# Two float32r parts in place of one float32 matmul for GpSimd's sum of exponentials, issued one step later

## The chip, the cores and the metric

One core of a Trainium2 chip. The metric is device time in microseconds (us); the kernel before has a median of 3220.47 us over 3 runs (3214.39 to 3221.25). TensorE is called PE, VectorE DVE, ScalarE ACT, GpSimd POOL, and the queue that issues the transfers SP. Each engine works its own queue in order.

## The reference, cut to what matters

A hybrid encoder layer for 2048 prompt tokens and 512 sample tokens, width 1024. One input projection feeds two attention mixers of 8 heads each: branch A (grouped-query, head size 64) and branch B (latent attention, 64 + 32). Both attend without a mask inside their own group of tokens:

```
s = jnp.einsum('bqgrd,bkgd->bgrqk', qblk, k, preferred_element_type=jnp.float32) * scale
p = jax.nn.softmax(s, axis=-1).astype(v.dtype)
return jnp.einsum('bgrqk,bkgd->bqgrd', p, v)
```

The two results are gated, projected, merged, projected once more, normalised and added to x. All of it is float32. Softmax needs, for each query, the sum of its exponentials over all keys: this sum is what the change is about.

## The kernel before, in words

Three stages follow one another: `in_proj` (about 1160 us), `attention` (to about 2750 us) and `tail`. The change touches `attention` alone.

**Float32 from float32r.** TensorE's float32r form rounds its operands. So the kernel splits a float32 operand into a rounded high part and a low part, the difference, and multiplies the parts in several matmuls. ScalarE makes the high part (a copy whose output is float32r), VectorE or GpSimd subtracts to get the low one.

**Jobs and steps.** Attention is 80 jobs: branch by branch, head by head, and in each head four chunks of 512 prompt queries and one chunk of 512 sample queries. A prompt job has 2048 keys, cut into 16 key tiles of 128; a *step* takes two of them, so a prompt job has 8 steps (n = 0 to 7) and a sample job 2. In each step:

- PE writes the scores of the step's two key tiles into a PSUM tile `st` (line 980; two matmuls per key tile in branch A, three in branch B). `st` has two buffers.
- ACT writes `ph`, the rounded exponential, to SBUF (line 983; a ring of six buffers), and then the full exponential back into `st` (line 984).
- DVE subtracts the two into `pl`, the low part (line 993). That frees `st`.
- PE also computes scores for a coming job into `mp` (line 947, one buffer), and DVE takes their maximum (line 950): the maximum has to be known before a job's own exponentials.
- Two to three steps later PE multiplies `ph` and `pl` with the values (`values`, lines 1003 and 1004) into the PSUM tiles `X` and `Y` of the job, one buffer each. `values` for the last key tile of a job stands in the next job's second step, and for the first tiles in a job's own fourth step.

**The sum of the rounded weights.** Y's row 64 collects the sums over keys. The low parts come in through a column of ones in the value tile (line 1004). The rounded parts of pairs n = 0 to 6 are added by POOL: six adds of 128x1024 into `acc` (line 986) and one that adds the two halves of `acc` (line 988). They enter Y through one float32 matmul with a selector, `sel[0]` (line 1008), right behind the job's last values. The last pair, n = 7, is summed by PE itself with the float32r selector `sel[1]` (line 1006, two matmuls). Sample jobs use line 1006 for all their tiles and have no `acc`.

**The end of a job.** `finish` has ACT copy X and Y to SBUF (lines 1015 and 1016); POOL then adds the two halves of X's copy (line 1027, tile `xa`) and, after a transfer, a second piece (line 1029, tile `s`). `later(k, f)` posts work k steps on.

**What sets the order.** From the first job on, the order of PE, ACT, DVE, POOL and SP is the order in which the Python loop at the end of `attention` emits the instructions: in each step first `scores`, then the values that have come due with one step of the maximum stream (`advance`) among them, then what `later` has due, then `lows`, then the POOL add that `finish` returned.

Of the kernel before, what the change touches and what calls it, by code (L numbers as in the profile page):

```python
# [9 lines left out]
F32 = mybir.dt.float32  # L10
F32R = mybir.dt.float32r
AF = mybir.ActivationFunctionType
ALU = mybir.AluOpType
# [4 lines left out]
P = 128  # L18
# [5 lines left out]
CH = 512  # L24
# [119 lines left out]
VW = 130  # L144
# [614 lines left out]
def attention(tc, nc, env, h4):  # L759
    e = NS(env)  # L760
    dma, nm, f32 = e.dma, e.nm, e.f32
    ha, fl, filler, cur, rest = h4
    kp = Pool(tc, "kp", "left")
# [21 lines left out]
    def zero_q(pool):  # L785
        qz = pool.tile([P, CH], F32R, name=nm("qz"))
        nc.vector.memset(f32(qz), 0.0)
        qzs.append(qz)

    zero_q(kp)  # L790
    zero_q(kp)
    sel = [kp.tile([P, VW - 64], t, name=f"sel{n}") for n, t in enumerate((F32, F32R))]
    for a in (sel[0], f32(sel[1])):
        nc.vector.memset(a, 0.0)
        nc.vector.memset(a[:, 64:VW - 64], 1.0)
    tops = [[kp.tile([P, 32], F32, name=f"m{s}{n}") for s in "pt"] for n in range(3)]
    for m, _ in tops:
        nc.vector.memset(m, 0.0)
# [35 lines left out]
    def post_now(out, in_):  # L834
        dma(f32(out), in_)
# [7 lines left out]
    def start(i, br, h, c):  # L843

        j = Job()
        j.br, j.h, j.c = br, h, c
        j.last = (br, h, c) == specs[-1]
        smp = int(c == 4)
        j.nk = (NS_TOK if smp else NP_TOK) // P
        j.direct = 0 if smp else j.nk // 2 - 1  # L850
        j.k1, j.k2, j.vt = kcur[(*kv_of(br, h), smp)]
        j.k3 = k3s[smp]
        qn, qr = q_src(br, h, c)
        j.qz = qzs[i % 3]
        j.qm = kp.tile([P, CH], F32R, tag="qm", name=nm("qm"), bufs=4)
        if br == 0:
            dma(f32(j.qm), qn[0].partition_broadcast(2))
            j.km = j.k1
            j.scale = SC_A
        else:  # L860
            dma(f32(j.qm[0:64, :]), qn[0])
            dma(f32(j.qm[64:128, :]), qr[0].partition_broadcast(2))
            j.km = j.k2
            j.scale = SC_B
        j.mx = kp.tile([P, 4, 2], F32, tag="mx", name=nm("mx"), bufs=3)
        return j
# [15 lines left out]
    at = Pool(tc, "at", "left")  # L882
# [35 lines left out]
    jobs = []  # L918
# [7 lines left out]
    def due(last=False):  # L926
        while queue and (last or queue[0][0] <= clock[0]):
            queue.pop(0)[2]()
# [37 lines left out]
            later(1, row)  # L966
            yield True

    def scores(j, n):

        if n == 0:
            if j.direct:
                j.acc = at.tile([P, 2, CH], F32, tag="acc", name=nm("acc"), bufs=2)
            j.hs, j.ls = [], []
        st = pp.tile([P, 2, CH], F32, tag="st", name=nm("st"), bufs=2)
        for a in range(2):
            kt = 2 * n + a
            ps = j.passes(j, slice(kt * P, (kt + 1) * P))
            for i, (k, q) in enumerate(ps):
                nc.tensor.matmul(st[:, a, :], lhsT=k, rhs=q, start=(i == 0), stop=(i == len(ps) - 1))  # L980
        h = at.tile([P, 2, CH], F32R, tag="ph", name=nm("ph"), bufs=6)
        j.hs.append(h)
        nc.scalar.activation(out=h, in_=st, func=AF.Exp, scale=j.scale)  # L983
        nc.scalar.activation(out=st, in_=st, func=AF.Exp, scale=j.scale)  # L984
        if 0 < n < j.direct:
            nc.gpsimd.tensor_tensor(out=j.acc, in0=f32(j.hs[0]) if n == 1 else j.acc, in1=f32(h), op=ALU.add)  # L986
            if n == j.direct - 1:
                nc.gpsimd.tensor_tensor(out=j.acc[:, 0, :], in0=j.acc[:, 0, :], in1=j.acc[:, 1, :], op=ALU.add)
        return st

    def lows(j, st):
        l = at.tile([P, 2, CH], F32R, tag="pl", name=nm("pl"), bufs=4)
# [3 lines left out]
    def values(j, kt):  # L996

        if kt == 0:
            j.X, j.Y = x_bank(), y_bank()
        n, a = kt // 2, kt % 2  # L1000
        y = j.Y[0:VW - 64, :]
        st, sp = kt == 0, kt == j.nk - 1
        nc.tensor.matmul(j.X, lhsT=j.vt[:, kt, 0:P], rhs=j.hs[n][:, a, :], start=st, stop=sp)  # L1003
        nc.tensor.matmul(y, lhsT=j.vt[:, kt, 64:VW], rhs=j.ls[n][:, a, :], start=st, stop=False)  # L1004
        if n >= j.direct:
            nc.tensor.matmul(y, lhsT=sel[1], rhs=j.hs[n][:, a, :], start=False, stop=sp and not j.direct)  # L1006
        if sp and j.direct:
            nc.tensor.matmul(y, lhsT=sel[0], rhs=j.acc[:, 0, :], start=False, stop=True)  # L1008
        return j if sp else None

    def finish(j):

        y = at.tile([VW - 64, CH], F32, tag="y", name=nm("ys"), bufs=2)
        xa = at.tile([P, CH], F32, tag="xa", name=nm("xa"), bufs=2)
        nc.scalar.copy(out=xa, in_=j.X)  # L1015
        nc.scalar.copy(out=y, in_=j.Y[0:VW - 64, :])
        later(1, lambda: dma(e.sums[j.br][j.c, j.h:j.h + 1, :], y[64:65, :]))
        if j.h == 7 and not j.last:
            for k, step in enumerate(inverse(nc, e, at, j.br, j.c)):
                later(6 + 2 * k, step)  # L1020
        if (j.br, j.h, j.c) == (1, 7, 0):
            for k, step in enumerate(tail_load(nc, e, wt, 1, 0, first_y)):
                later(13 + 3 * k, step)

        def rest():
            s = at.tile([64, CH], F32, tag="s", name=nm("s"), bufs=2)
            nc.gpsimd.tensor_tensor(out=xa[0:64, :], in0=xa[0:64, :], in1=y[0:64, :], op=ALU.add)
            later(1, lambda: dma(s, xa[64:128, :]))
            later(3, lambda: nc.gpsimd.tensor_tensor(out=s, in0=s, in1=xa[0:64, :], op=ALU.add))
            later(5, lambda: dma(  # L1030
                e.o_s[j.br][j.h // 2, 64 * (j.h % 2):64 * (j.h % 2) + 64, j.c * CH:(j.c + 1) * CH], s))

        return rest
# [4 lines left out]
    def advance(to):  # L1038
        while done[0] < to and next(stream, None) is not None:
            done[0] += 1  # L1040

    steps = [(i, n) for i, m in enumerate(pairs) for n in range(m)]
# [3 lines left out]
    with contextlib.ExitStack() as order:  # L1046
# [14 lines left out]
        passes = {0: start_main(0, *specs[0])}  # L1061
        order.close()
        order.enter_context(tc.manual_schedule(engines={eng.PE, eng.Activation, eng.DVE, eng.Pool, eng.SP}))
        ready, g = [], -1
        while g + 1 < len(steps) or ready:
            g += 1
            clock[0] = g
            st, rest = None, None
            if g < len(steps):
                i, n = steps[g]  # L1070
                br, h, c = specs[i]
                if c < 2 and n == 4:
                    late = [0]

                    def post_later(out, in_):
                        later(late[0], lambda: post_now(out, in_))
                        late[0] += 1

                    if c == 0 and i + 5 < len(specs):
                        load_k(*kv_of(*specs[i + 5][0:2]), 0, post_later)  # L1080
                    if c == 1:
                        load_k(*kv_of(br, h), 1, post_later)
                if n == 0:
                    for k in range(i + 1, min(i + 3, len(specs))):
                        if k not in passes and (k == i + 1 or pairs[i + 1] < 8):
                            passes[k] = start_main(k, *specs[k])
                    jobs[i].passes = passes.pop(i)
                    if specs[i] == (1, 0, 0):
                        for k in range(4):
                            later(24 * k + 4, lambda k=k: wa.append(load_raw(nc, e, wt, e.a_out, k)))  # L1090
                            later(24 * k + 12, lambda k=k: wa.append(
                                split_raw(nc, e, wt, "wa", wa.pop(), k, nc.gpsimd)))
                        for m, step in enumerate(tail_load(nc, e, wt, 0, 0, first_y)):
                            later(24 * m + 100, step)
                        later(180, lambda: y0.extend(split_y(nc, e, wt, 0, first_y.pop())))
                st = scores(jobs[i], n)
                ready += [(g + BACK + (n == 0), jobs[i], 2 * n + a) for a in range(2)]
            now = sum(r[0] <= g for r in ready)
            for m in range(min(now, 3)):
                if m == 1:  # L1100
                    advance(lead + g + 1)
                _, j, kt = ready.pop(0)
                if values(j, kt):
                    rest = finish(j)
            if now < 2:
                advance(lead + g + 1)
            due()
            if st is not None:
                lows(jobs[i], st)
            if rest:  # L1110
                rest()
# [217 lines left out]
```

## Time and profile before

| what | value |
|---|---|
| median of 3 runs | 3220.47 us |
| the profiled execution's own time | 3216.27 us |
| its span | 3214.5 us |
| PE busy over the span | 3146.4 us, 98% |
| DVE, ACT, POOL busy over the span | 60%, 51%, 57% |
| granted TensorE clock, mean | 0.994 |
| branch A, 32 prompt and 8 sample jobs | about 1226 to 1925 us |
| branch B, the same number of jobs | about 1925 to 2745 us |

The shares over the span are averages over three stages; inside `attention` they are different, and the two branches differ from each other since branch B has two more score matmuls in each step. A busy PE is not a PE at its peak: its matmuls overlap, each is recorded with about 390 ns, and they start some 230 ns apart. What a matmul takes of PE's time is therefore read from the starts.

### The profile page before, as it was taken

The page shows a single profiled execution, that of the slowest core. Times are in us where ns is not written, and L with a number is a line of the kernel's source. Part 1 is how long each engine was busy: PE and PEld are TensorE (multiplying, and loading weights), DVE is VectorE, ACT ScalarE, POOL GpSimd, SP SyncE. Part 2 cuts the span into 40 slices and gives each one's busy share as a digit, 9 for nine tenths or more (in the row PEclk, how much of TensorE's full clock was granted, in tenths as well). Part 3 has the DMA queues.
Part 4 walks back from the last instruction along what each step waited for, and adds up shares of the span by engine and source line. Part 5 has one row for each costly group of instructions (what it writes and reads, how often), then busy time and mean ns, then how long its engine had stood idle before and what let it go on. Part 6 is the DMA issues. An engine that isn't in the chain of part 4 may idle for free.

```text
span 3214.5 us, 41877 instructions
## 1 busy us (share of the span) xinstructions
PE 3146.4 (98%) x15214; PEld 2538.8 (79%) x15214; DVE 1919.8 (60%) x2441; ACT 1635.3 (51%) x2169; POOL 1820.4 (57%) x1124
## 2 busy tenths in 40 slices
PE   7999999999999989999999999999999999899999
PEld 6988889988889877777777777777777777799997
DVE  5733214532205227999999998887887887544443
ACT  5332234232224226888888877777676777321122
POOL 6422123421224336888888887777776778644443
PEclk9999999999999999999999999999999999999999
DMA  8445542365634741112111134433433222665552
GB/s 244 146 150 204 189 159 90 120 201 180 205 103 151 223 144 55 40 37 68 42 48 36 38 88 105 99 91 84 94 93 86 67 66 69 197 190 164 162 175 73
DMA packets 283922, 383.89 MB, mean 119 GB/s; under 512 B 31916, under 2 KB 185844, under 8 KB 281252
## 3 DMA queue, kind: packets, MB, share of 16 engines
q1 hardware_dynamic: 283716, 381.22, 40.1%
q8 instruction: 120, 1.97, 0.3%
q14 instruction: 86, 0.70, 0.1%
HBM read 251.52 MB, written 118.96 MB: 115 GB/s over the span
## 4 chain that ended last, share of the span: by engine, by line
PE 87%; DMA 4%; DVE 3%; issue 2%; ACT 2%; POOL 1%; SPq 1%; ACTq 0%; POOLq 0%; DVEq 0%
PE st L980 18%; PE mm L604 17%; PE mm L340 8%; PE mp L947 8%; PE py L1004 7%; PE pv L1003 7%; PE z L1270 6%; PE ab L1204 6%; PE mm L692 3%; PE py L1008 2%; PE py L1006 1%; SPq L44 1%; PE pv L604 1%; DMA raw<-in_w_in 1%; PE py L604 1%
## 5 line engine op out<-in xcount | busy, mean ns | idle before, releaser
L986 POOL TENSOR_TENSOR acc<-acc,ph 128x1024 f32<-128x1024 f32 x320 | 768.8, 2403 | 56.1 <-ACT ph L983 42.0
L950 DVE TENSOR_REDUCE mx<-mp 128x1 f32<-128x1024 f32 x512 | 625.9, 1222 | 218.1 <-PE mp L947 217.1
L983 ACT ACTIVATE ph<-st 128x1024 fp32r<-128x1024 f32 x544 | 558.5, 1027 | 364.7 <-PE st L980 357.0
L993 DVE TENSOR_TENSOR pl<-st,ph 128x1024 fp32r<-128x1024 f32 x544 | 658.2, 1210 | 37.9 <-ACT st L984 37.5
L984 ACT ACTIVATE st<-st 128x1024 f32<-128x1024 f32 x544 | 555.5, 1021 | 0.0
L209 POOL TENSOR_TENSOR wl<-wraw,wh 128x1536 fp32r<-128x1536 f32 (+3 forms) x59 | 189.0, 3214 | 508.8 <-ACT wh L208 508.2
L980 PE MATMUL st<-qm,k 128*128 128x512 f32 x1024 | 434.1, 424 | 9.1 <-DVE pl L993 8.4
L980 PE MATMUL st<-qz,k 128*128 128x512 f32 x1056 | 416.1, 394 | 0.0
L1003 PE MATMUL pv<-ph,vt 128*128 128x512 f32 x1024 | 404.3, 395 | 4.0 <-ACT xa L1015 3.6
L1004 PE MATMUL py<-pl,vt 128*66 128x512 f32 x1024 | 404.7, 395 | 0.0
L947 PE MATMUL mp<-k,qm 128*128 128x512 f32 x1024 | 323.4, 397 | 0.4 <-DVE mx L950 0.4
L604 PE MATMUL mm<-hh,wh 128*128 128x512 f32 x768 | 302.2, 394 | 0.0
L604 PE MATMUL mm<-hl,wh 128*128 128x512 f32 x768 | 301.8, 393 | 0.0
L604 PE MATMUL mm<-hh,wl 128*128 128x512 f32 x768 | 301.8, 393 | 0.0
L980 PEld LDWEIGHTS st<-qm,k 128*128 128x128 f32 x1024 | 192.2, 188 | 110.2 <-DVE pl L993 35.8
L947 PEld LDWEIGHTS mp<-k,qm 128*128 128x128 f32 x1024 | 190.6, 188 | 73.4 <-DVE mx L950 11.9
L986 POOL TENSOR_TENSOR acc<-ph,ph 128x1024 f32<-128x1024 f32 x64 | 153.0, 2390 | 161.7 <-ACT ph L983 161.7
L1003 PEld LDWEIGHTS pv<-ph,vt 128*128 128x128 f32 x1024 | 192.6, 188 | 61.8 <-ACT xa L1015 10.6
L980 PEld LDWEIGHTS st<-qz,k 128*128 128x128 f32 x1056 | 198.5, 188 | 47.6 <-issue 7.4
L340 PE MATMUL mm<-wh,hh 128*128 128x384 f32 (+1 forms) x640 | 210.9, 330 | 5.1 <-ACT hh L60 2.7
L340 PE MATMUL mm<-wl,hh 128*128 128x384 f32 (+1 forms) x640 | 210.1, 329 | 0.0
L340 PE MATMUL mm<-wh,hl 128*128 128x384 f32 (+1 forms) x640 | 205.8, 330 | 0.0
(235 smaller groups left out, 5782.5 us busy)
## 6 DMA issues: line engine op xcount, KB each, us to landing
wraw<-in_w_in SPq DMA_DIRECT2D x46, 768.0 KB
x<-in_x_prompt SPq DMA_DIRECT2D x32, 512.0 KB
wada<-in_ada_w SPq DMA_DIRECT2D x24, 512.0 KB
raw<-in_w_in SPq DMA_DIRECT2D x48, 256.0 KB
vb<-uv SPq DMA_DIRECT2D x20, 512.0 KB
qm<-aqh SPq DMA_DIRECT2D x40, 256.0 KB
s<-xa SPq DMA_DIRECT2D x80, 128.0 KB
mt<-ma SPq DMA_DIRECT2D x40, 256.0 KB
```

The costliest lines, as they stand in the source:

```text
L340: nc.tensor.matmul(ps[:, 0:n], lhsT=lt, rhs=rt, start=(i == 0), stop=(i == 23))
L604: nc.tensor.matmul(ps, lhsT=lt, rhs=rt[:, k, :], start=(i == 0), stop=(i == 23))
L947: nc.tensor.matmul(mp[:, a, :], lhsT=j.qm[:, qt * P:(qt + 1) * P], rhs=j.km[:, kc * CH:(kc + 1) * CH], start=True, stop=True)
L950: nc.vector.tensor_reduce(out=j.mx[:, n // 2, n % 2:n % 2 + 1], in_=mp.rearrange("p a k -> p (a k)"), axis=AX.X, op=ALU.max)
L980: nc.tensor.matmul(st[:, a, :], lhsT=k, rhs=q, start=(i == 0), stop=(i == len(ps) - 1))
L983: nc.scalar.activation(out=h, in_=st, func=AF.Exp, scale=j.scale)
L984: nc.scalar.activation(out=st, in_=st, func=AF.Exp, scale=j.scale)
L986: nc.gpsimd.tensor_tensor(out=j.acc, in0=f32(j.hs[0]) if n == 1 else j.acc, in1=f32(h), op=ALU.add)
L993: nc.vector.tensor_tensor(out=l, in0=st, in1=f32(j.hs[-1]), op=ALU.subtract)
L1003: nc.tensor.matmul(j.X, lhsT=j.vt[:, kt, 0:P], rhs=j.hs[n][:, a, :], start=st, stop=sp)
L1004: nc.tensor.matmul(y, lhsT=j.vt[:, kt, 64:VW], rhs=j.ls[n][:, a, :], start=st, stop=False)
L1204: nc.tensor.matmul(ps[:, dd, :], lhsT=a, rhs=b, start=(i == 0), stop=(i == 11))
```

## The change

- At the first step of the job that follows a prompt job (`sum_parts`, called from `scores` between its two exponentials) ACT copies the summed half of `acc` into a float32r tile `hl`, and POOL writes the remainder of that rounding into the tile's second half. `hl` takes a place in the ring of six that `ph` uses.
- The float32 matmul of line 1008 is gone. Instead `sums` issues two float32r matmuls, one for each part, one step after the job's last values: in the third step of the next job (behind a sample job's two steps, in the first step of the job after it).
- `finish` is cut in two. X is copied where it was; the copy of Y and all that hangs on it (`finish_sums`) come one step later, behind the two new matmuls.
- One selector, float32r, is left.

```diff
-    def scores(j, n):
+    def scores(j, n, ended):
...
         nc.scalar.activation(out=h, in_=st, func=AF.Exp, scale=j.scale)
+        if ended:
+            sum_parts(ended)
         nc.scalar.activation(out=st, in_=st, func=AF.Exp, scale=j.scale)
...
+    def sum_parts(j):
+
+        a = j.acc[:, 0, :]
+        j.sum = at.tile([P, 2, CH], F32R, tag="ph", name=nm("hl"), bufs=6)
+        nc.scalar.copy(out=j.sum[:, 0, :], in_=a)
+        nc.gpsimd.tensor_tensor(out=j.sum[:, 1, :], in0=a, in1=f32(j.sum[:, 0, :]), op=ALU.subtract)
...
         if n >= j.direct:
-            nc.tensor.matmul(y, lhsT=sel[1], rhs=j.hs[n][:, a, :], start=False, stop=sp and not j.direct)
-        if sp and j.direct:
-            nc.tensor.matmul(y, lhsT=sel[0], rhs=j.acc[:, 0, :], start=False, stop=True)
+            nc.tensor.matmul(y, lhsT=sel, rhs=j.hs[n][:, a, :], start=False, stop=sp and not j.direct)
         return j if sp else None
 
+    def sums(j):
+        for k in range(2):
+            nc.tensor.matmul(j.Y[0:VW - 64, :], lhsT=sel, rhs=j.sum[:, k, :], start=False, stop=k == 1)
+
     def finish(j):
 
+        j.xa = at.tile([P, CH], F32, tag="xa", name=nm("xa"), bufs=2)
+        nc.scalar.copy(out=j.xa, in_=j.X)
+
+    def finish_sums(j):
+
+        xa = j.xa
         y = at.tile([VW - 64, CH], F32, tag="y", name=nm("ys"), bufs=2)
-        xa = at.tile([P, CH], F32, tag="xa", name=nm("xa"), bufs=2)
-        nc.scalar.copy(out=xa, in_=j.X)
         nc.scalar.copy(out=y, in_=j.Y[0:VW - 64, :])
...
-                st = scores(jobs[i], n)
+                st = scores(jobs[i], n, jobs[i - 1] if i and n == 0 and jobs[i - 1].parts else None)
...
                 if values(j, kt):
-                    rest = finish(j)
+                    finish(j)
+                    if j.parts:
+                        ending.append((g + 1, j))
+                    else:
+                        rest = finish_sums(j)
             if now < 2:
                 advance(lead + g + 1)
+            if ending and ending[0][0] == g:
+                j = ending.pop(0)[1]
+                sums(j)
+                rest = finish_sums(j)
```

How the instructions stand now, at the end of the first job (branch A). Rows of the change have the changed kernel's line numbers: its exponentials are lines 983 and 986, POOL's adds into `acc` line 988, the sum of halves line 990. First ACT's queue, from the next job's first exponential on; `ph_10840` of the rows before and `ph_10837` of the rows now are that job's first step. Before:

```order
L983 ACTIVATE ph_10840<-st_10835 128x1024
L984 ACTIVATE st_10835<-st_10835 128x1024
L983 ACTIVATE ph_10858<-st_10853 128x1024
L984 ACTIVATE st_10853<-st_10853 128x1024
L1015 COPY xa_10874<-pv_10732 128x512
L1016 COPY ys_10873<-py_10733 66x512
L983 ACTIVATE ph_10886<-st_10881 128x1024
L984 ACTIVATE st_10881<-st_10881 128x1024
```

And in the change:

```order
L983 ACTIVATE ph_10837<-st_10832 128x1024
L997 CAST hl_10839<-acc_10675 128x512
L986 ACTIVATE st_10832<-st_10832 128x1024
L983 ACTIVATE ph_10858<-st_10853 128x1024
L986 ACTIVATE st_10853<-st_10853 128x1024
L1025 COPY xa_10872<-pv_10729 128x512
L983 ACTIVATE ph_10881<-st_10876 128x1024
L986 ACTIVATE st_10876<-st_10876 128x1024
L1031 COPY ys_10891<-py_10730 66x512
```

The new cast stands between the two exponentials of the first step, and the copy of Y (`ys`) has moved behind those of the third step.

POOL's queue over the same job, from one sum of halves to the next. Before:

```order
L988 TENSOR_TENSOR acc_10678<-acc_10678 128x512
L986 TENSOR_TENSOR acc_10834<-ph_10840,ph_10858 128x1024
L1027 TENSOR_TENSOR xa_10874<-xa_10874,ys_10873 64x512
L986 TENSOR_TENSOR acc_10834<-acc_10834,ph_10886 128x1024
L986 TENSOR_TENSOR acc_10834<-acc_10834,ph_10903 128x1024
L986 TENSOR_TENSOR acc_10834<-acc_10834,ph_10928 128x1024
L1029 TENSOR_TENSOR s_10879<-s_10879,xa_10874 64x512
L986 TENSOR_TENSOR acc_10834<-acc_10834,ph_10955 128x1024
L986 TENSOR_TENSOR acc_10834<-acc_10834,ph_10975 128x1024
L988 TENSOR_TENSOR acc_10834<-acc_10834 128x512
```

And in the change:

```order
L990 TENSOR_TENSOR acc_10675<-acc_10675 128x512
L998 TENSOR_TENSOR hl_10839<-acc_10675,hl_10839 128x512
L988 TENSOR_TENSOR acc_10831<-ph_10837,ph_10858 128x1024
L988 TENSOR_TENSOR acc_10831<-acc_10831,ph_10881 128x1024
L1042 TENSOR_TENSOR xa_10872<-xa_10872,ys_10891 64x512
L988 TENSOR_TENSOR acc_10831<-acc_10831,ph_10902 128x1024
L988 TENSOR_TENSOR acc_10831<-acc_10831,ph_10929 128x1024
L988 TENSOR_TENSOR acc_10831<-acc_10831,ph_10955 128x1024
L1044 TENSOR_TENSOR s_10895<-s_10895,xa_10872 64x512
L988 TENSOR_TENSOR acc_10831<-acc_10831,ph_10976 128x1024
L990 TENSOR_TENSOR acc_10831<-acc_10831 128x512
```

POOL has one instruction more in each prompt job, the subtraction into `hl`, and the adds `xa` and `s` stand one add of `acc` later.

PE's queue in the change, from the last values of the first job to the first values of the second:

```order
L1015 MATMUL py_10730<-ph_10814,sel 66x512
L980 MATMUL st_10876<-qm_10318,k_9395 128x512
L980 MATMUL st_10876<-qz_9415,k_9396 128x512
L980 MATMUL st_10876<-qm_10318,k_9395 128x512
L980 MATMUL st_10876<-qz_9415,k_9396 128x512
L947 MATMUL mp_10885<-k_9395,qm_10633 128x512 x2
L1020 MATMUL py_10730<-hl_10839,sel 66x512 x2
L980 MATMUL st_10897<-qm_10318,k_9395 128x512
L980 MATMUL st_10897<-qz_9415,k_9396 128x512
L980 MATMUL st_10897<-qm_10318,k_9395 128x512
L980 MATMUL st_10897<-qz_9415,k_9396 128x512
L1012 MATMUL pv_10906<-ph_10837,vt_9397 128x512
```

Before, the float32 matmul stood right behind the first of these rows; now two float32r ones stand behind the third step's scores and maxima. In branch B each group of score matmuls has six rows in place of four.

## Rows read from the trace of the kernel before

**Rows 1.** Busy time by stretch: branch A, branch B (header row names the columns).

```profile
core 0: us, PE busy (x) PEld busy (x) DVE busy (x) ACT busy (x) POOL busy (x), PEclk, DMA share, GB/s
1226.00:1925.00 699.00, 691.20 (x2859) 493.82 (x2858) 642.98 (x615) 562.55 (x617) 595.62 (x300) 1.00 0.19 49
1925.00:2745.00 820.00, 812.24 (x3419) 604.92 (x3418) 649.11 (x616) 575.80 (x637) 621.08 (x313) 1.00 0.35 85
```

**Rows 2.** Timeline of PE, branch B, end of a prompt job (start, us, instruction).

```profile
2082.12 0.40 PE L1006 MATMUL py<-ph,sel 128*66 128x512 f32 x1
2082.35 1.02 PE L1008 MATMUL py<-acc,sel 128*66 128x512 f32 x2
...
2083.45 0.39 PE L980 MATMUL st<-q,k 128*128 128x512 f32 x1
```

**Rows 3.** Timeline of POOL, branch A, one prompt job.

```profile
1354.98 1.29 POOL L988 TENSOR_TENSOR acc<-acc 128x512 f32<-128x512 f32 x1
1357.95 2.38 POOL L986 TENSOR_TENSOR acc<-ph,ph 128x1024 f32<-128x1024 f32 x1 [1.69 <-ACT ph L983]
1360.29 1.30 POOL L1027 TENSOR_TENSOR xa<-xa,ys 64x512 f32<-64x512 f32 x1
1361.66 7.37 POOL L986 TENSOR_TENSOR acc<-acc,ph 128x1024 f32<-128x1024 f32 x3
1368.99 1.29 POOL L1029 TENSOR_TENSOR s<-s,xa 64x512 f32<-64x512 f32 x1
1370.24 4.87 POOL L986 TENSOR_TENSOR acc<-acc,ph 128x1024 f32<-128x1024 f32 x2
1375.19 1.30 POOL L988 TENSOR_TENSOR acc<-acc 128x512 f32<-128x512 f32 x1
```

**Rows 4.** Timeline of ACT, branch A, the same prompt job.

```profile
1354.52 1.03 ACT L983 ACTIVATE ph<-st 128x1024 fp32r<-128x1024 f32 x1 [0.39 <-PE st L980]
1355.44 1.02 ACT L984 ACTIVATE st<-st 128x1024 f32<-128x1024 f32 x1
1356.85 1.02 ACT L983 ACTIVATE ph<-st 128x1024 fp32r<-128x1024 f32 x1 [0.39 <-PE st L980]
...
1374.95 1.03 ACT L983 ACTIVATE ph<-st 128x1024 fp32r<-128x1024 f32 x1 [0.37 <-PE st L980]
```

**Rows 5.** Groups by line, shapes apart: a cast and a subtraction of 128x512 elsewhere.

```profile
L628 POOL TENSOR_TENSOR fl<-raw,fh 128x512 fp32r<-128x512 f32 x48 | 61.7, 1300 | 111.3 <-ACT fh L627 111.2
...
L627 ACT CAST fh<-raw 128x512 fp32r<-128x512 f32 x48 | 29.0, 620 | 74.7 <-DMA raw<-in_w_in 57.1 <-PE mm L604 16.8
```

**Rows 6.** Timeline of POOL, branch A, a sample job and the prompt job after it.

```profile
1307.39 1.30 POOL L988 TENSOR_TENSOR acc<-acc 128x512 f32<-128x512 f32 x1
...
1316.59 2.40 POOL L986 TENSOR_TENSOR acc<-ph,ph 128x1024 f32<-128x1024 f32 x1 [2.00 <-ACT ph L983]
...
1335.56 1.30 POOL L988 TENSOR_TENSOR acc<-acc 128x512 f32<-128x512 f32 x1
```

**Rows 7.** Line 988 in branch A: count, durations, first and last start.

```profile
L988 POOL TENSOR_TENSOR acc<-acc x32: 1282/1295/1306, 1245.2 to 1923.3; 128x512 f32<-128x512 f32 x32
```

**Rows 8.** Timeline of ACT and POOL, branch B, end of a prompt job.

```profile
2099.68 1.30 POOL L988 TENSOR_TENSOR acc<-acc 128x512 f32<-128x512 f32 x1
...
2101.53 1.02 ACT L983 ACTIVATE ph<-st 128x1024 fp32r<-128x1024 f32 x1 [0.84 <-PE st L980]
```

**Rows 9.** Timeline, branch B, the step after a sample job's last values.

```profile
2137.31 0.40 PE L980 MATMUL st<-qz,k 128*128 128x512 f32 x1
...
2137.80 1.02 ACT L983 ACTIVATE ph<-st 128x1024 fp32r<-128x1024 f32 x1 [2.02 <-PE st L980]
...
2139.66 0.59 ACT L1015 COPY xa<-pv 128x512 f32<-128x512 f32 x1
...
2140.30 0.19 PEld L1003 LDWEIGHTS pv<-ph,vt 128*128 128x128 f32 x1 [0.49 <-ACT xa L1015]
```

**Rows 10.** Line 1008: what PE waited for before it (us, times).

```profile
  POOL acc L988: 3.5, 2
```

More of the change, by code (lines that the diff above doesn't have):

```diff
@@ L791, in attention @@
     zero_q(kp)
[L792 to L795, printed above, removed]
+    sel = kp.tile([P, VW - 64], F32R, name="sel")
+    nc.vector.memset(f32(sel), 0.0)
+    nc.vector.memset(f32(sel[:, 64:VW - 64]), 1.0)
     tops = [[kp.tile([P, 32], F32, name=f"m{s}{n}") for s in "pt"] for n in range(3)]
@@ L849, in start @@
         j.nk = (NS_TOK if smp else NP_TOK) // P
+        j.parts = not smp
         j.direct = 0 if smp else j.nk // 2 - 1
@@ L1063, in attention @@
         order.enter_context(tc.manual_schedule(engines={eng.PE, eng.Activation, eng.DVE, eng.Pool, eng.SP}))
-        ready, g = [], -1
-        while g + 1 < len(steps) or ready:
+        ready, ending, g = [], [], -1
+        while g + 1 < len(steps) or ready or ending:
             g += 1
```

## The prediction

> **What bounds the kernel now.** The change touches attention alone, so I read the busy time of its two branches first [rows 1]. In branch B PE is busy for 812 of 820 us: PE is the bound, and what is taken from PE there is worth its own length. In branch A PE is busy for 691 of 699 us by the records, but their ends are modelled; DVE is busy for 643 us (92%) and POOL for 596 us (85%), so two other engines stand close behind, and a saving on PE need not come through. Then I read PE at a job's end for the price of the float32 matmul [rows 2], and POOL's and ACT's queues over one job of branch A for the new dependence between them [rows 3, 4].
>
> What the reader is to see in the last two: in branch A POOL runs late. Its sum of halves (line 988) starts at 1354.98 and so ends at 1356.27 [rows 3], while ACT has finished the next job's first rounded exponential at 1354.52 + 1.03 = 1355.55 and goes on at once with the second exponential [rows 4]. Nobody minds before: the float32 matmul that reads the sum stands a whole step later on PE. From line 988 on POOL then idles until the second exponential pair of the new job (1.69 us [rows 3]) and so catches up once per job; for the rest of the job its queue is full, from 1357.95 to the next line 988 at 1375.19.
>
> **The change, part by part.**
>
> *PE's work.* Matmuls of one pass start 0.23 us apart (2082.12 to 2082.35). From the start of the float32 matmul to the second score matmul behind it are 2083.45 - 2082.35 = 1.10 us, of which the first score matmul has 0.23, so the float32 one costs 0.87 [rows 2]. Two float32r matmuls cost 0.46. Where PE is the bound that saves 0.41 us for each of 64 prompt jobs, 26 us in all.
> The Trainium skill (TensorE: Matmul & The Clock Gate, Back-to-back issue gap) gives about 131 ns per matmul of 512 columns in a stream of weight loads and matmuls. By it the pair would cost 0.26 us and the saving would be 0.61 a job; no row here comes near it, so I stay with 0.23.
>
> *ACT's new cast, the decisive part.* It stands between the first step's two exponentials, and it needs POOL's sum of halves, line 988. ACT works in order: while the cast waits, the full exponential behind it waits, DVE's low part (line 993) behind that, and the score buffer `st` that it would free, which PE needs for the third step. Before, the sum of job j was needed by nobody before the second step's end; now POOL and ACT form a closed loop from one job to the next: line 988, cast, full exponential, second rounded exponential, POOL's first add of the new job (it needs that exponential), five more adds with `xa` and `s` among them, line 988 again. Its length in branch A:
> - line 988 takes 1.30, and POOL starts 0.08 after an ACT instruction it needs (1356.85 + 1.02 = 1357.87 to 1357.95 [rows 3, 4]); I take 0.08 in the other direction too;
> - the cast: an equal one, 128x512 to float32r, takes 0.62 [rows 5]. ACT starts an instruction some 0.1 before the last one's end (1354.52 to 1355.44 is 0.92 for one of 1.03 [rows 4]), so 0.52 from cast to full exponential, 0.92 to the rounded one, 1.02 for that, 0.08 to POOL: 2.54;
> - first add to line 988, without a gap of note: 1357.95 to 1375.19 is 17.24 [rows 3]. The same eight instructions stand there in the change.
> Sum 1.30 + 0.08 + 2.54 + 17.24 = 21.16, say 21.2 us per prompt job, against 1375.19 - 1354.98 = 20.21 now. POOL's new subtraction (1.30 [rows 5]) lies inside the 2.54: it starts 0.70 after the cast began and ends at 2.0, so it costs nothing while the first add waits for ACT; without that cover it would be 1.3 a job.
> Across a sample job the same loop is longer: line 988 to the first add of the next prompt job takes 1316.59 - 1307.39 = 9.20 now, and 9.4 with the cast ahead of ACT's work there (I take 0.2 of its 0.5, since ACT has waits there), and then 18.97 to line 988 [rows 6], in all 28.4 against 28.2.
> Branch A has 32 sums of halves, from 1245.2 to 1923.3: 678.1 us [rows 7], with 24 short ways and 7 long ones between them. In the change 24 x 21.2 + 7 x 28.4 = 708. **Branch A loses 30 us.** Its saving on PE (13 us) does not come out, since PE is then no longer the bound; what PE waits for is the score buffer. Bounds: if POOL's first add followed the subtraction at once (1.30 + 0.08 + 0.62 + 0.08 + 1.30 + 0.07 = 3.45 from line 988) the loop would be 20.7 and branch A 17 us slower; if ACT's third exponential pair comes too late for POOL's second add, where `xa` no longer fills the gap, I allow 0.3 on every way and 0.5 on the long ones, 12 us more.
>
> *Branch B.* A prompt job is longer there, since PE has two more score matmuls per key tile pair, and POOL keeps up: line 988 ends at 2100.98, the next job's first rounded exponential at 2102.55, 1.57 us later [rows 8]. Two adds move back by one place, and `s` (1.29) now stands right ahead of the last add; that leaves about 0.3 us. So the cast does not wait in a usual job of branch B, and a wait of up to half a microsecond would be covered, because PE wants the score buffer only after the next step's work. The saving of 0.41 counts: 32 x 0.41 = 13 us.
> Against it, the copy of Y. It now stands behind the third step's exponentials, and the first matmul into the next Y (line 1004 in the fourth step) must wait for it, with all of PE's queue. The sample jobs show this form already: from the last score matmul's start 0.49 to the rounded exponential, 1.86 more to the copy, 0.59 for it, 0.05 to PE [rows 9]. From the start of the third step's scores that is 5 x 0.23 + 2.99 = 4.15 us; PE arrives there after 6 scores, 2 maxima, 2 sums, 6 scores and one value matmul, 17 x 0.23 = 3.93. So 0.22 us of each 0.41 goes again, 32 x 0.22 = 7 us. In the rows the weight load after a sample job sits 0.49 idle for its copy, which would take all of it: bounds 0 and 16 us.
> A few jobs of branch B share POOL with work for the last stage (weights to split, a tile to scale), and there the sum comes late: before, PE waited for it twice, 3.5 us in all [rows 10]. A late sum now holds up ACT a step earlier; I put 6 us on this, with 0 and 12 as its ends. **Branch B: -13 + 7 + 6 = 0.**
>
> *The rest.* `hl` takes a place in the ring of six `ph`. A tile's place is reused six tiles later; with one more tile per job the distance shrinks by one step where `hl` lies between, but POOL's adds of those tiles are done three steps earlier. Nothing. The memset that goes is setup.
>
> **Sum.** 3216.3 (the profiled execution's own time) + 30 + 0 = 3246. The median of the runs is 4.2 above that execution; the time to be compared will have the same scatter, and I give **3249 us**, about 0.9% slower.
>
> **The rivals.**
> *The saving comes through in both branches.* If ACT had its sum in time everywhere, 64 x 0.41 = 26 us less, and some 3 us of waits on Y given back: about 3193. It decides by whether line 988 ends before the cast's turn. For it: POOL's share in branch A is 85%, so there is room on average. Against it: the ends 1356.27 and 1355.55, and the loop that cannot be shorter than 20.7 where a job now takes 20.2. Chance 0.12.
> *A wash.* The late sum costs only the lateness seen now (0.7 us a job in rows 3 and 4, half of it covered as in branch B), since ACT's wait also lets POOL catch up; with PE's 0.41 against it A comes to nearly nothing, and B to -6 to 0: 3214 to 3224. Against it: POOL's first add waits for ACT, so a waiting ACT gives POOL nothing. Chance 0.08.
> *The loop closes in branch B as well,* where the 0.3 left there is eaten by POOL's adds and by the jobs that share POOL: half a microsecond beyond the cover for each of 32 jobs is 16 us more, 3265. Inside my forecast's upper end.
>
> **How the numbers follow.** The forecast, slower by the loop in branch A, has 0.80. Its own range: A from 17 to 42, B from -13 to 15, hardly both ends at once, so 3228 to 3272. To leave out no more than 2 in 10 I reach down into the wash: 3216 to 3270. A difference under 0.2% (6.4 us) cannot be told from none here. Faster by more: 0.13 (the first rival and a corner of the wash); within: 0.07; slower by more: 0.80.
>
> **What would show it.** Right: in branch A ACT's cast begins after a wait for POOL's sum of halves, in nearly all 32 jobs, one to two us each, and the starts of the sums of halves lie about 21.2 and 28.4 apart; PE idles for DVE's `pl` (line 993) at the third step; in branch B the sums are some 0.2 us a job closer than now, and PE shows short waits for the copy of Y. Wrong: casts that start right behind the exponential in branch A, sums of halves that stay 20.2 apart or come closer, or a branch B that ends 10 us earlier or later than now.

## The result and the profile after

| | before | the change |
|---|---|---|
| median of 4 runs | 3219.05 us | 3257.51 us (3256.98 to 3258.95) |
| the profiled execution's own time | 3216.27 us | 3258.95 us |
| its span | 3214.5 us | 3257.1 us |

The change makes the kernel slower: a ratio of 1.0122, 95% interval 1.011 to 1.0135. It is 38 us by the medians and 42.6 us by the spans of the two profiled executions (the one of before lies near the lower end of its runs, the one of the change is the slowest of its four).

First the page of the changed kernel: PE's busy time, and the chain that ended last, by engine.

```profile
PE 3152.5 (97%) x15214; PEld 2533.3 (78%) x15214; DVE 1922.9 (59%) x2439; ACT 1663.4 (51%) x2233; POOL 1903.0 (58%) x1188
...
PE 64%; POOL 16%; ACT 5%; DMA 5%; issue 4%; DVE 4%; SPq 1%; POOLq 0%; ACTq 0%; DVEq 0%
```

The chain of the page before, by engine:

```profile
PE 87%; DMA 4%; DVE 3%; issue 2%; ACT 2%; POOL 1%; SPq 1%; ACTq 0%; POOLq 0%; DVEq 0%
```

PE is busy for as long as before (3146 us then), in a longer span. What is new is POOL, with 16% of the chain in place of 1%. Where that lies is read from the sum of halves (line 990 of the changed kernel, line 988 of the kernel before [rows 7]). This is the view of one line: count, least, median and longest duration in ns, first and last start; under it who waited for the line (us in total, times). Branch A:

```profile
L990 POOL TENSOR_TENSOR acc<-acc x32: 1282/1292/1304, 1246.8 to 1957.6; 128x512 f32<-128x512 f32 x32
...
  ACT hl L997: 31.8, 31
```

Branch B:

```profile
L990 POOL TENSOR_TENSOR acc<-acc x32: 1262/1295/1307, 1987.1 to 2777.1; 128x512 f32<-128x512 f32 x32
...
  ACT hl L997: 10.6, 5
```

And branch B of the kernel before:

```profile
L988 POOL TENSOR_TENSOR acc<-acc x32: 1264/1290/1302, 1952.4 to 2740.5; 128x512 f32<-128x512 f32 x32
```

From the first sum to the last, branch A takes 1957.6 - 1246.8 = 710.8 us in place of 678.1 [rows 7], **32.7 us more**, and branch B 790.0 in place of 788.1, 1.9 us more. In branch A the cast `hl` waited for the sum 31 times, 31.8 us in all. The end of attention follows from the last copy of Y. The copy's line in the changed kernel, and in the kernel before:

```profile
L1031 ACT COPY ys<-py x80: 579/584/591, 1254.5 to 2787.9; 66x512 f32<-66x512 f32 x80
```

```profile
L1016 ACT COPY ys<-py x80: 581/583/587, 1251.0 to 2746.4; 66x512 f32<-66x512 f32 x80
```

From the last sum to the start of that copy it is 2787.9 - 2777.1 = 10.8 us in place of 2746.4 - 2740.5 = 5.9, 4.9 us more. The rest of the 42.6 us is spread: 1.6 ahead of the first sum, 0.4 between the branches, 1.1 behind attention.

That end is ACT's queue again. After the last sum, in the change and then in the kernel before (start, us, instruction, idle time ahead of it and what ended it):

```profile
2778.44 0.62 ACT L997 CAST hl<-acc 128x512 fp32r<-128x512 f32 x1 [5.29 <-POOL acc L990]
2781.75 0.59 ACT L1025 COPY xa<-pv 128x512 f32<-128x512 f32 x1
2782.39 0.80 PE L1012 MATMUL pv<-ph,vts 128*128 128x512 f32 x1 [1.24 <-ACT xa L1025]
```

```profile
2741.81 1.07 PE L1008 MATMUL py<-acc,sel 128*66 128x512 f32 x2 [1.51 <-POOL acc L988]
2742.32 0.80 PE L1003 MATMUL pv<-ph,vts 128*128 128x512 f32 x1
```

The cast waits 5.29 us for the sum. Behind it stand three exponentials and the copy of X, which PE's next value matmul needs: that one starts 2782.39 - (2777.15 + 1.26) = 3.98 us after the sum has ended, in place of 2742.32 - (2740.49 + 1.26) = 0.57. PE had stood idle for 3.01 us at the first of the new matmuls, 0.66 at the second and 1.24 here, and the granted clock of the stretch that follows is 0.50, the level of 1.2 GHz; in the kernel before it is 1.00 there. The two stretches, with the columns of [rows 1]:

```profile
2782.30:2787.50 5.20, 5.11 (x12) 3.24 (x13) 1.04 (x2) 0.95 (x3) 1.27 (x1) 0.50 0.15 32
2742.00:2746.00 4.00, 3.56 (x14) 1.83 (x14) 0.21 (x1) 0.63 (x2) 1.28 (x1) 1.00 0.20 42
```

In them the sample job's twelve matmuls start 0.43 us apart, in place of some 0.24.

The loop itself, in branch A. POOL's timeline over one prompt job, which answers to [rows 3] (start, us, instruction, idle time ahead of it and what ended it):

```profile
1360.86 1.29 POOL L990 TENSOR_TENSOR acc<-acc 128x512 f32<-128x512 f32 x1
1362.88 1.30 POOL L998 TENSOR_TENSOR hl<-acc,hl 128x512 fp32r<-128x512 f32 x1 [0.73 <-ACT hl L997]
1364.74 2.39 POOL L988 TENSOR_TENSOR acc<-ph,ph 128x1024 f32<-128x1024 f32 x1 [0.56 <-ACT ph L983]
1367.48 2.40 POOL L988 TENSOR_TENSOR acc<-acc,ph 128x1024 f32<-128x1024 f32 x1 [0.36 <-ACT ph L983]
1369.85 1.28 POOL L1042 TENSOR_TENSOR xa<-xa,ys 64x512 f32<-64x512 f32 x1
1371.10 7.36 POOL L988 TENSOR_TENSOR acc<-acc,ph 128x1024 f32<-128x1024 f32 x3
1378.40 1.30 POOL L1044 TENSOR_TENSOR s<-s,xa 64x512 f32<-64x512 f32 x1
1379.65 2.42 POOL L988 TENSOR_TENSOR acc<-acc,ph 128x1024 f32<-128x1024 f32 x1
1382.15 1.29 POOL L990 TENSOR_TENSOR acc<-acc 128x512 f32<-128x512 f32 x1
```

ACT's timeline at the same job's first steps, which answers to [rows 4]:

```profile
1360.09 1.03 ACT L983 ACTIVATE ph<-st 128x1024 fp32r<-128x1024 f32 x1 [0.36 <-PE st L980]
1362.19 0.62 ACT L997 CAST hl<-acc 128x512 fp32r<-128x512 f32 x1 [1.07 <-POOL acc L990]
1362.71 1.01 ACT L986 ACTIVATE st<-st 128x1024 f32<-128x1024 f32 x1
1363.65 1.01 ACT L983 ACTIVATE ph<-st 128x1024 fp32r<-128x1024 f32 x1
```

And DVE's:

```profile
1360.96 1.23 DVE L950 TENSOR_REDUCE mx<-mp 128x1 f32<-128x1024 f32 x1
1363.75 1.23 DVE L1002 TENSOR_TENSOR pl<-st,ph 128x1024 fp32r<-128x1024 f32 x1 [1.57 <-ACT st L986]
```

ACT has done its rounded exponential at 1361.12, and then stands idle for 1.07 us until the sum of halves (1360.86 + 1.29 = 1362.15); the cast starts at 1362.19. The second exponential, which nobody had to hold, starts at 1362.71, and DVE's low part behind it waits 1.57 us. POOL's first add then waits for ACT's next rounded exponential (0.56 us), not for its own subtraction. From one sum of halves to the next are 1382.15 - 1360.86 = 21.29 us; it was 20.21 [rows 3]. The loop is closed, and it is POOL and ACT that go round in it.

### The profile page after: what moved, and what is told of

Read it like the earlier page. It is cut to its first block, busy times and chain, and to the rows that moved or that the text cites. A ratio compares the mean times of both kernels' runs of the same rounds, so it can differ in the third digit from the quotient of the medians.

```text
span 3257.1 us, 42145 instructions
## 1 busy us (share of the span) xinstructions
PE 3152.5 (97%) x15214; PEld 2533.3 (78%) x15214; DVE 1922.9 (59%) x2439; ACT 1663.4 (51%) x2233; POOL 1903.0 (58%) x1188
## 4 chain that ended last, share of the span: by engine, by line
PE 64%; POOL 16%; ACT 5%; DMA 5%; issue 4%; DVE 4%; SPq 1%; POOLq 0%; ACTq 0%; DVEq 0%
PE mm L604 16%; PE st L980 11%; POOL acc L988 11%; PE mm L340 8%; PE ab L1227 6%; PE z L1293 6%; PE py L1013 4%; PE pv L1012 4%; PE mp L947 3%; PE mm L692 3%; ACT st L986 2%; POOL s L1044 2%; DVE pl L1002 2%; POOL acc L990 1%; ACT ph L983 1%
## 5 line engine op out<-in xcount | busy, mean ns | idle before, releaser
L209 POOL TENSOR_TENSOR wl<-wraw,wh 128x1536 fp32r<-128x1536 f32 (+3 forms) x59 | 189.1, 3216 | 508.6 <-ACT wh L208 508.0
L980 PE MATMUL st<-qm,k 128*128 128x512 f32 x1024 | 414.2, 405 | 35.3 <-DVE pl L1002 34.6
L980 PE MATMUL st<-q,k 128*128 128x512 f32 x512 | 203.0, 396 | 0.0
```

## The experiments

All edits are against the changed kernel. Ratios are to the kernel before. "A" is the stretch from the first to the last sum of halves in branch A, "B" that in branch B; before they are 678.1 and 788.1, in the change 710.8 and 790.0. The time is the median of a version's runs; A and B are read from its one profiled execution, which for the first experiment is the fastest of ten, 7 us under their median.

| run | median us | ratio, 95% | A | B |
|---|---|---|---|---|
| the change | 3257.5 | 1.011 to 1.0135 | 710.8 | 790.0 |
| cast behind the second exponential | 3225.0 | 1.0008 to 1.0028 | 682.7 | 785.9 |
| branch B alone | 3224.1 | 1.0008 to 1.0027 | 677.2 | 789.4 |
| sums at the head of the step | 3253.5 | 1.0093 to 1.0123 | 711.8 | 785.0 |
| no low part | 3254.7 | 1.0096 to 1.013 | 710.9 | 790.2 |
| late cast and early sums | 3219.1 | 0.9994 to 1.0012 | 685.3 | 781.4 |
| the same, branch B alone | 3214.4 | 0.9983 to 1.0001 | 676.6 | 780.7 |
| six pairs on POOL in branch A | 3237.9 | 1.005 to 1.0077 | 690.8 | 789.8 |
| the same, early sums | 3221.6 | 1.0006 to 1.0024 | 679.3 | 785.7 |
| branch B alone, weights split by DVE | 3225.5 | 1.0016 to 1.0037 | 678.0 | 789.2 |

### The cast one place later

```diff
         nc.scalar.activation(out=h, in_=st, func=AF.Exp, scale=j.scale)
+        nc.scalar.activation(out=st, in_=st, func=AF.Exp, scale=j.scale)
         if ended:
             sum_parts(ended)
-        nc.scalar.activation(out=st, in_=st, func=AF.Exp, scale=j.scale)
```

> The cast of the sum stands behind the first step's second exponential instead of ahead of it; nothing else moves. Theory (the loop line 990, cast, exponentials, first add of acc, line 990 through ACT sets branch A): the cast leaves the loop's ACT part between the two exponentials and has 0.92 us more before its turn, so the short way is 1.30 + 0.03 + 0.52 + 1.02 + 0.08 + 17.3 = 20.3 us in place of 21.3, and sums of halves in branch A span about 24 x 20.3 + 7 x 27.9 = 682 us in place of 711: about 29 us less than the change, 3228. Rival 1 (the later copy of Y holds PE up; that wait is 37 us in the change) and rival 2 (POOL simply has too much work) and rival 3 (the ring of six is too short with hl in it): none of them is touched, so 3257 within 6.

Measured: 3225.0 us, 32.5 less than the change. Branch A's sums, and who waited for them:

```profile
L990 POOL TENSOR_TENSOR acc<-acc x32: 1277/1291/1302, 1243.3 to 1926.0; 128x512 f32<-128x512 f32 x32
...
  ACT hl L997: 11.2, 23
```

Every instruction of the change is still there, in another order on ACT alone, and 28 of branch A's 33 us are gone: A is 682.7, as the loop's length foretold. The cast still waits a little in 23 jobs, 11 us in all, so the loop still sets the pace, but of 20.4 us a job. Branch B, where a few casts waited too, gives back 4.1 us more. The three rivals foresaw no gain; they cannot hold the main part of the loss.

### Branch B alone

```diff
-        j.parts = not smp
+        j.parts = not smp and br == 1
...
+        if sp and j.direct and not j.parts:
+            nc.tensor.matmul(y, lhsT=sel0, rhs=j.acc[:, 0, :], start=False, stop=True)
         return j if sp else None
```

> Branch A keeps the float32 matmul and its old places, branch B has the change (both selectors are there). Theory: the loss of 33 us in branch A goes whole, branch B keeps its few us: 3221 to 3227, branch A's sums of halves 678 us apart from first to last. Rival 1 (the later copy of Y, which costs the same wait in each branch): half of the loss stays, 3238. Rival 2 (POOL overloaded everywhere): 3238 or so as well.

Measured: 3224.1 us. Branch A's sums:

```profile
L992 POOL TENSOR_TENSOR acc<-acc x32: 1285/1294/1306, 1245.0 to 1922.2; 128x512 f32<-128x512 f32 x32
```

A is 677.2, as before the change, and the time lies 14 us under the 3238 of both rivals. The loss of branch A is its own, and branch B alone with the change as written still loses 0.2%.

### The sums at the head of the third step

```diff
             st, rest = None, None
+            if ending and ending[0][0] == g:
+                j = ending.pop(0)[1]
+                sums(j)
+                rest = finish_sums(j)
             if g < len(steps):
...
-            if ending and ending[0][0] == g:
-                j = ending.pop(0)[1]
-                sums(j)
-                rest = finish_sums(j)
             due()
```

> The two matmuls and the copy of Y stand at the head of the next job's third step, ahead of its scores and exponentials, instead of at its end; the cast stays where the change has it. Theory: branch A is set by the loop and stays (711 us from first to last sum), the waits for the copy of Y (37 us in all) go, and only those of branch B were worth anything, 0.2 to 0.4 us for 32 jobs: 3244 to 3251. Rival 1 (the later copy of Y is what costs): the whole 37 us come back, 3220. Rival 2: 3257.

Measured: 3253.5 us, 4 us less than the change, 2.5 above the range that the theory gave and far from the rival's 3220. Branch A's and branch B's sums:

```profile
L990 POOL TENSOR_TENSOR acc<-acc x32: 1279/1292/1300, 1244.3 to 1956.1; 128x512 f32<-128x512 f32 x32
```

```profile
L990 POOL TENSOR_TENSOR acc<-acc x32: 1259/1293/1305, 1985.2 to 2770.2; 128x512 f32<-128x512 f32 x32
```

A stays at 711.8: in branch A the waits for the copy of Y cost nothing as long as the loop is longer than what PE needs. B falls from 790.0 to 785.0. So the later copy of Y has a price in branch B, 5 us, close to the 7 us of the prediction.

### No low part

The low part of the sum is not made; the sum enters rounded.

```diff
         nc.scalar.copy(out=j.sum[:, 0, :], in_=a)
-        nc.gpsimd.tensor_tensor(out=j.sum[:, 1, :], in0=a, in1=f32(j.sum[:, 0, :]), op=ALU.subtract)
...
-        for k in range(2):
-            nc.tensor.matmul(j.Y[0:VW - 64, :], lhsT=sel, rhs=j.sum[:, k, :], start=False, stop=k == 1)
+        nc.tensor.matmul(j.Y[0:VW - 64, :], lhsT=sel, rhs=j.sum[:, 0, :], start=False, stop=True)
```

> The low part of the sum is left out: no subtraction on POOL, one matmul instead of two; the cast stays. Theory: POOL's first add of a job waits for ACT's second rounded exponential and not for the subtraction, so the loop is as long as before in branch A (21.3 us, 711 in all), and branch B gains at most the matmul, 32 x 0.23 = 7 us, and some POOL slack: 3247 to 3257. Rival 2 (POOL has too much work, 64 x 1.3 = 83 us added): most of the loss goes, 3225 or less. Rival 1: 3257.

Measured: 3254.7 us. Branch A's sums:

```profile
L990 POOL TENSOR_TENSOR acc<-acc x32: 1283/1292/1308, 1245.6 to 1956.5; 128x512 f32<-128x512 f32 x32
...
  ACT hl L997: 31.8, 31
```

POOL does 64 instructions of 1.3 us less, 83 us of busy time, and A does not move by a tenth: 710.9, with the same 31.8 us of waiting. POOL's load as such is not the cause: this part of it lay beside the loop, under ACT's work. What counts is the way around, on which POOL and ACT wait for each other.

### A shorter loop with the cast where it was

```diff
-        j.direct = 0 if smp else j.nk // 2 - 1
+        j.direct = 0 if smp else j.nk // 2 - (2 if br == 0 else 1)
```

POOL now sums six pairs of a job in branch A, its sum of halves stands one step earlier, and one pair more enters TensorE directly.

> The change as it is, the cast where the change has it, but in branch A POOL adds six pairs instead of seven (one add of 128x1024 less in its part of the loop) and PE sums two more key tiles with the selector (0.46 us a job). Theory: POOL's part of the loop falls by 2.45 us to 18.9, below what DVE and PE need (20.1 to 20.3), so ACT's cast no longer waits and branch A returns to about 680 us from first to last sum: 3257 - 31 = 3226, within 5. Rival (it is ACT's extra 0.62 us between the exponentials, or the later copy of Y, that stretches a job, and not the wait on POOL): no gain, 3257, or 15 us more by PE's extra matmuls.

Measured: 3237.9 us, between the two forecasts, 12 above the theory's. Branch A's sums (nobody waited for them), and from the who-waits view of branch A what PE waited for at the copy of Y (us in total, times, longest us):

```profile
L990 POOL TENSOR_TENSOR acc<-acc x32: 1288/1298/1308, 1241.3 to 1932.1; 128x512 f32<-128x512 f32 x32
```

```profile
PEld py L1013 <- ACT ys L1031: 26.2, 38, 0.8
PE py L1013 <- ACT ys L1031: 10.8, 31, 0.4
```

The wait on the sum is gone altogether and 20 of the 33 us with it, though the cast still stands between the two exponentials. The other 13 were left: once the loop no longer covers it, PE's wait for the copy of Y is on the path in branch A too, or PE's two additional matmuls are. The next run tells the two apart.

### The shorter loop with the sums early

Both edits, this one and the one of the sums at the head of the step.

> The run with six pairs on POOL in branch A, with the two sums and the copy of Y at the head of the third step as well. It tells what the 13 us are that branch A of that run (691 us from first to last sum of halves) still lay above the kernel before (678). If they are PE's wait for the copy of Y (37 us of recorded waits there, part of them hidden): they go, branch A about 680, the time 3238 - 10 - 5 = 3223. If they are the two more matmuls on PE (32 x 0.46 = 15 us): branch A stays at 690, the time 3233.

Measured: 3221.6 us. Branch A's sums:

```profile
L990 POOL TENSOR_TENSOR acc<-acc x32: 1292/1297/1302, 1243.8 to 1923.1; 128x512 f32<-128x512 f32 x32
```

A is 679.3, though PE still has the two more matmuls. So 11.5 of the 13 us were the late copy of Y, and 1.2 are left. In the change as it stands they were hidden under the loop. PE's work in a job of this version is close to what it was before, 0.46 us more for the two key tiles and 0.41 less for the sum; over 32 jobs that is 1.6 us, near the 1.2 measured.

### Late cast and early sums

The edit of the first run and that of the third together: the cast behind the second exponential, and the sums at the head of the step.

> Both moves together in both branches: the cast behind the first step's second exponential, the two sums and the copy of Y at the head of the third step. Theory: the two effects are separate, so they add: the cast's move gives branch A back 28 us (short way 20.4 between sums of halves), the early sums give branch B some 5 us (usual short way 23.45 to 23.25, long way 30.6 to 30.1): 3225 - 5 = 3220, within 4. Rival (with the sums early PE waits for hl in branch A, 0.5 us or more a job, as the waits of e3 for hl hint): branch A back at 690 us or more between first and last sum, 3228 or more.

Measured: 3219.1 us, within 0.1% of the kernel before and 38.4 us less than the change; the two moves alone gave 32.5 and 4.0. Branch A's sums:

```profile
L990 POOL TENSOR_TENSOR acc<-acc x32: 1287/1294/1302, 1243.5 to 1928.8; 128x512 f32<-128x512 f32 x32
...
  ACT hl L997: 23.0, 31
```

The cast waits in all 31 jobs here, 23 us in all, so at 685.3 branch A still goes by the loop, 2.6 us longer than with the late cast alone. This is a part of what the rival named, well short of its 690. The saving on PE comes out in branch A in no version; one with the saving, without the loop and without additional matmuls was not run.

### The same, in branch B alone

Those two edits and that of the second run.

> Branch A as before the change, branch B with the parts, the late cast and the early sums. Theory: branch A 678 us from first to last sum of halves; branch B loses its waits for the copy of Y and most of ACT's waits for late sums, and keeps the 0.4 us of PE in each prompt job: 3224 (branch B alone as changed) - 5 - 4 = 3215, 4 us below the kernel before. Rival (branch B's few late sums, behind POOL's work for the last stage, cost what PE saves, wherever the cast stands): 3220 to 3224.

Measured: 3214.4 us, a ratio of 0.9992 with an interval from 0.9983 to 1.0001: the best version of all, 3 us under the kernel before, but not clear of it. Branch B's sums:

```profile
L992 POOL TENSOR_TENSOR acc<-acc x32: 1261/1297/1309, 1949.6 to 2730.3; 128x512 f32<-128x512 f32 x32
...
  ACT hl L999: 8.6, 5
```

B is 780.7 in place of 788.1. Five casts still wait, 8.6 us in all, 4.8 of them at the last sum.

### The last stage's weights split by DVE

```diff
-                                split_raw(nc, e, wt, "wa", wa.pop(), k, nc.gpsimd)))
+                                split_raw(nc, e, wt, "wa", wa.pop(), k, nc.vector)))
```

This is on top of the version for branch B alone.

> The version with the parts in branch B alone, late cast and early sums, and with the four low parts of the last stage's first weights (2.4 us each) made by DVE instead of POOL, since POOL's late sums are what is left of the loss in branch B. If those four are behind the late sums: 2 to 4 us less than 3214, 3211. If it is other work on POOL (the tile scaled twice for the last stage) or a late transfer: 3214, or a little more where DVE is then late.

Measured: 3225.5 us, 11 us worse than without it; a miss. Branch B's sums:

```profile
L992 POOL TENSOR_TENSOR acc<-acc x32: 1262/1297/1308, 1954.3 to 2743.5; 128x512 f32<-128x512 f32 x32
...
  ACT hl L999: 5.6, 2
```

Fewer casts wait (2 for 5), but B is 789.2, 8.5 us longer. What the four subtractions did in DVE's queue, here the first, and PE's next score matmul:

```profile
1969.67 2.65 DVE L1174 TENSOR_TENSOR wal<-raw,wah 128x1024 fp32r<-128x1024 f32 x1 [0.90 <-ACT wah L1173]
1973.51 0.50 PE L982 MATMUL st<-qm,k 128*128 128x512 f32 x1 [2.29 <-DVE pl L1004]
```

DVE reaches three of the four before ACT has made their high part (`wah`) and waits 0.90, 1.57 and 1.32 us for it, then works on the four for 2.65, 1.98, 1.72 and 1.47 us. `pl` stands behind them, and PE waits for it 2.29, 2.26, 2.24 and 1.15 us, 7.9 us in all, nearly the whole 8.5. It is the fault of the change once more: an instruction with a late operand, ahead of one that PE waits for.

## Why the prediction was right

It gave 3249 us (3216 to 3270) and slower; 3257.5 was measured. By its own steps:

- **The loop, branch A.** Forecast 21.2 us from sum to sum and 28.4 across a sample job, 30 us for the branch. Measured 21.29 in the rows above, 28.5 across a sample job, and 32.7 us for the branch; 31 casts waited, 0.4 to 1.7 us each. That it is a loop and not a load is shown: moving the cast by one place gives back 28 us, taking 83 us of work from POOL beside the loop gives back nothing, and shortening POOL's part of the loop takes all waiting away. ACT's cast starts 0.04 us after the sum ends (1362.15 to 1362.19) where 0.08 was taken, and POOL's second add waits 0.36 us for ACT, which the upper bound had allowed for.
- **POOL's subtraction costs nothing under its cover.** Right: the first add waits for ACT and not for it, and without it branch A is as long.
- **The saving on PE does not come out in branch A.** Right for the change. In branch A the chain that ended last then runs through POOL (its adds into `acc` are 43% of it) and no longer through PE. The shortest version with the parts, 679.3, is no shorter than before either, but PE has two more matmuls a job in it, so it does not tell what the saving would be worth without the loop.
- **The copy of Y, branch B.** Forecast 0.22 us a job. PE and ACT of the changed kernel at that place:

```profile
2122.64 0.39 PE L980 MATMUL st<-qz,k 128*128 128x512 f32 x1
2122.87 0.40 PE L1012 MATMUL pv<-ph,vt 128*128 128x512 f32 x1
2123.32 0.45 PE L1013 MATMUL py<-pl,vt 128*66 128x512 f32 x1
```

```profile
2122.68 0.59 ACT L1031 COPY ys<-py 66x512 f32<-66x512 f32 x1
```

  The first matmul into Y starts 2123.32 - 2122.87 = 0.45 after its neighbour, where 0.23 is usual: 0.22, as worked out. In all it was 5 us for the branch (sums early) against a forecast of 7.
- **Branch B as a whole: the term that was too small.** Forecast 0 (-13 + 7 + 6), measured 1.9 between its sums and 4.9 at its end. The starts of the sums of halves tell the terms apart. Here is a head in which no cast waits for a sum (from one sum to the fourth after it, with the sample job between), before, in the change, and with the sums early:

```profile
L988 POOL TENSOR_TENSOR acc<-acc x5: 1288/1290/1302, 2154.9 to 2256.1; 128x512 f32<-128x512 f32 x5
```

```profile
L990 POOL TENSOR_TENSOR acc<-acc x5: 1288/1295/1307, 2192.1 to 2292.9; 128x512 f32<-128x512 f32 x5
```

```profile
L990 POOL TENSOR_TENSOR acc<-acc x5: 1293/1295/1305, 2189.7 to 2289.2; 128x512 f32<-128x512 f32 x5
```

  It takes 101.2 us before, 100.8 in the change and 99.5 with the sums early, and two other such heads agree within 0.5 us. On the mean of the three, 0.39 us a job is saved with the sums early (forecast 0.41), of which the late place of the sums and of the copy of Y takes 0.27 (forecast 0.22). The 0.12 left would be 4 us over 32 jobs. That the branch takes 1.9 more puts the late sums at some 6 us (an estimate from these rows), as forecast; but the prediction did not see the 4.9 at the end, where the late sum holds ACT, the copy of X waits behind it and the granted clock falls to 0.50. Late sums and end together, between 10 and 11 us, lie inside its upper end of 12. This is the main reason why 3249 was low; by the two profiled spans, branch A took 2.7 us beyond its forecast and the stretches outside attention another 2.7.
- **The rivals.** The saving did not come through, and the wash did not happen: ACT's wait gives POOL nothing, as was argued against it. Nor did the loop close in branch B: 5 casts waited for their sum there, in branch A 31. Each of the five sums came behind a POOL instruction of 2.4 us for the last stage.

## What to carry to other kernels

An instruction that reads another engine's late result should be put in an in-order queue behind all that the rest of the kernel waits for; here one place in ACT's queue was worth 28 of the 33 us that branch A had lost. When a change makes two engines wait for each other once per round, add up the way around (instruction by instruction, with what must be waited for); if it is longer than the round now takes, that sum is the new round, however idle the two engines are on average. A saving on an engine is not paid out in a stage where the change itself makes another chain the longer one, as in branch A: look stage by stage before spending work of other engines on it.

## What was not expected of the hardware

Moving four subtractions of 2.4 us from POOL to DVE, where DVE's share is 79% in branch B [rows 1], cost 11 us in place of a gain. A share with room in it said nothing on whether the queue had a place for them: their high parts came late, and `pl`, for which PE waits, stood behind. And the same delay of the copy of Y had two prices: nothing in branch A as long as the loop was longer, and 11.5 us there (690.8 to 679.3) as soon as it was not. Last, a wait of a few us at the end of attention had a second price: PE's granted clock was 0.50 behind it, and twelve matmuls started 0.43 us apart.
